# Linear attention decode with keys on partitions, masked copies, roots by token, and column-tiled products issued behind their last operand

## The chip, the cores and the metric

The kernel runs on one core of one Trainium2 chip. The metric is the device time of one execution in microseconds (us), the median of several runs. Five engines run their own instruction queues side by side: TensorE (matmuls, PE in the profile), VectorE (DVE), ScalarE (ACT), GpSimd (POOL) and SyncE (SP), which here issues every DMA transfer.

## The reference, cut to what matters

One inference step of a decoder layer, in float32, for a new prompt (16 meta tokens and 256 tokens) and for one new token each of 8 running sequences. The normalized input is projected into three branches, a state-space scan (S5), gated linear attention (GLA) and attention over a local window of 128 (SWA); their results are gated, summed and projected, and a squared-ReLU MLP follows. The change touches GLA and one product of SWA. GLA has 4 heads with keys of 128 and values of 256. Prompt and decode compute:

```
lg = log_sigmoid(a_in @ w_gate2 + b_gate2) / 16
# prompt: the same recurrence in closed form, started from zero
# decode, for each sequence n and head h:
s = exp(lg)[..., None] * s + k[..., :, None] * v[..., None, :]
o = einsum('nhd,nhdv->nhv', q, s)
# both:
o = rmsnorm(o, g_out) * silu(r)          # over the 256 values of a head
```

The new decode state `s` is an output for each of the 8 sequences, 4 x 128 x 256 floats each. SWA ends in `o = einsum(p, v)` with softmaxed scores p.

## The kernel before, in words

Features lie on the 128 partitions and tokens run along the free axis: T = 280 columns (16 meta, 256 prompt, 8 decode) or NQ = 264 without meta tokens. Every large projection goes through `linear` (L144): `Weights.half` (L109 to L118) loads half a weight tile of 512 KB (`wraw`, L112), ScalarE rounds it into a high half (`whi`, L116), VectorE subtracts for the low half (`wlo`, L117), and `accumulate` (L130) multiplies three times, high by high, high by low and low by high. Nearly all of the kernel's matmuls are these. They need nothing of the branches until the branch outputs are projected, so projections of gates and queries run while the branches are computed.

The order of each engine's queue, SP's too, is fixed when the kernel is built: a scheduler walks the program with a time model of its own and takes, at each step, the ready instruction of highest priority. Priority is program order, raised where the code says `tc.high_priority`. On the chip each queue then runs in this order and waits where an operand is late. Tiles with a tag share `bufs` buffers, and a new tile waits until the old holder of its buffer is released.

GLA comes after the value projection (L623 to L640). `vt` holds prompt values with tokens on partitions, `vdc` (L630) decode values, `lg` the log gates. Then:

- Decode rows (L665 to L676): `dec3` gathers exp(lg), k and q of the decode tokens; TensorE transposes it, and it is written to a DRAM scratch `scr1`, so that it can be read back broadcast over all partitions.
- Prompt, eight levels (L706 to L747): at each level a q product `qt` (L713, GpSimd), a k product `ek` (L720, L725, VectorE), four products per half (L732), and the result multiplied by a mask (L736) and added into the attention matrix (L737), both on VectorE. Then the prompt's outputs go into `o_t` (L785), and the prompt's final state follows through `ku` (L794), four transposes a piece (L800) and L808.
- Decode (L814 to L829): 16 rounds, 8 sequences by two pairs of heads, with values on the partitions. Each loads broadcast rows (L817) and a state `s0` of 256 KB (L819), both in two buffers; GpSimd multiplies by the decay (L820); for each head and value half VectorE adds k times v (L825) and multiplies by q with a sum into `o_t` (L827); the state is stored (L829).
- Norm (L836 to L847): squares on ScalarE (L838), their sum on GpSimd (L839), a product with a matrix of ones that leaves the sum over partitions on every partition (L841), a copy (L842), one reciprocal root over 4 x 264 columns (`rsqrt`, L170 to L176), and the scaling of `o_t` (L847).
- Later `o_t` is multiplied by the gate `sr`, fetched from DRAM (L928, GpSimd), and split into high and low halves (L929, L930) for the branch's projection.

In SWA (the loop that ends at L1088, all at a raised priority) scores are transposed (L1076), copied to `pt`, and multiplied with the values by four products on four column tiles (L1082), two heads' operands in `pts[0]` and two in `pts[1]`.

Of the kernel before, what the change touches and what calls it, by code (L numbers as in the profile page):

```python
# [16 lines left out]
KT = D // 128  # L17
# [68 lines left out]
def trunk(tc, A):  # L86
# [68 lines left out]
    def C(name):  # L155
        a, n = CONST_COLS[name]
        return cst[:, a:a + n]
# [52 lines left out]
    vt = gproj.tile([128, 3, 8, 128], F32)  # L210
    vdc = gproj.tile([128, 8, DEC], F32)
    ab = gproj.tile([32, T], F32)
# [410 lines left out]
    for mm in range(4):  # L623
        vv = []
        for j in range(2):
            ps = linear(A['w_vb'][2 * mm + j], xpair, 0, T)
            vv.append(ev_tile())
            with tc.high_priority():
                V.tensor_mul(vv[j], ps[:, :T], r1)
            V.tensor_copy(vdc[:, 2 * mm + j], vv[j][:, TP:])  # L630
        ps = ps_side('A')
# [17 lines left out]
    with tc.tile_pool(name="lgp", bufs=1, side="right") as lp:  # L649
# [10 lines left out]
        S.activation(lab, lab, AF.Ln, bias=ones[:, 0:1])  # L660
        V.tensor_sub(lg, lg, lab)
    IT = 1.0 / 16.0


    dec3 = gmain.tile([128, DEC, 2, 3, 2], F32)  # L665
    for i in range(2):
        h2 = slice(2 * i, 2 * i + 2)
        S.activation(dec3[:, :, i, 0].rearrange("p n g -> p g n"), lg[:, h2, TP:], AF.Exp, scale=IT)
        V.tensor_copy(dec3[:, :, i, 1].rearrange("p n g -> p g n"), kb[:, h2, TP:])
        V.tensor_copy(dec3[:, :, i, 2].rearrange("p n g -> p g n"), qb[:, h2, SEQ:])  # L670
    ps = ps_side()
    PE.transpose(ps[:96, :128], dec3.rearrange("p n i z g -> p (n i z g)"), ident)
    drow = gmain.tile([96, 128], F32, name="drow", tag="rows", bufs=2)
    S.copy(drow, ps[:96, :128])
    scr1 = tc.dram_tile([DEC, 2, 6 * DK], F32, name="scr1")
    SY.dma_start(scr1.rearrange("n i (z d) -> (n i z) d", d=DK), drow)  # L676

# [25 lines left out]

    lvm = C('lvmask').rearrange("p (l t) -> p l t", l=7)
    eq, ek = None, None
    for lev in range(8):  # L706
# [5 lines left out]
        S.activation(eq.rearrange("p g (b h) -> p g b h", h=h), right, AF.Exp, scale=IT)  # L712
        P.tensor_mul(qt.rearrange("p g (b h) -> p g b h", h=h), eq.rearrange("p g (b h) -> p g b h", h=h),  # L713
                     qp.rearrange("p g (b two h) -> p g b two h", two=2, h=h)[:, :, :, 1, :])
# [12 lines left out]
        if lev < 7:  # L727
            for i in range(2):
                ps = ps_side()
                psv = ps[:, :GH * 64].rearrange("p (g t) -> p g t", g=GH)  # L730
                for hd in range(GH):
                    PE.matmul(psv[:, hd], kt[:, hd, 128 * i:128 * i + 128], qt[:, hd, 64 * i:64 * i + 64],  # L732
                              start=True, stop=True)
                dst = att_tile(i).rearrange("p g (b two h) -> p g b two h", two=2, h=h)[:, :, :, 1, :]
                msk = gp.tile([128, GH, 64], F32, name="msk", tag="msk")
                V.tensor_mul(msk, psv, lvm[:, lev][:, None, :].to_broadcast([128, GH, 64]))  # L736
                V.tensor_add(dst, dst, msk.rearrange("p g (b h) -> p g b h", h=h))  # L737
        else:
# [73 lines left out]


    for n in range(DEC):  # L814
        for i in range(2):
            rows = gmain.tile([128, 3, 2, DK], F32, name="rows", tag="rows", bufs=2)
            SY.dma_start(rows, bass.AP(tensor=scr1.tensor, offset=scr1[n, i].offset, ap=[[0, 128], [1, 6 * DK]]))  # L817
            s0 = gmain.tile([128, 2, 2, DK], F32, name="s0", tag="s0", bufs=2)
            SY.dma_start(s0, A['gla0'][n, :, 2 * i:2 * i + 2])  # L819
            P.tensor_mul(s0, s0, rows[:, 0][:, :, None, :].to_broadcast([128, 2, 2, DK]))  # L820
            scrap = gmain.tile([128, DK], F32, name="scrap", tag="scrap", bufs=1)
            for j in range(2):
                for vh in range(2):
                    m = 2 * (2 * i + j) + vh
                    V.scalar_tensor_tensor(s0[:, j, vh], rows[:, 1, j], vdc[:, m, n:n + 1], s0[:, j, vh],  # L825
                                           op0=OP.mult, op1=OP.add)
                    V.scalar_tensor_tensor(scrap, s0[:, j, vh], 1.0, rows[:, 2, j], op0=OP.mult, op1=OP.mult,  # L827
                                           accum_out=o_t[:, m, SEQ + n:SEQ + n + 1])
            SY.dma_start(A['o_sgla'][n, :, 2 * i:2 * i + 2], s0)  # L829


    gpx.close()
    gp = gpx.enter_context(tc.tile_pool(name="gla5", bufs=1, side="right"))
    rg = gp.tile([128, GH, NQ], F32)
    rsv = gp.tile([128, 3, GH, NQ], F32)
    for hd in range(GH):  # L836
        sq = gp.tile([128, 2, NQ], F32, name="osq", tag="osq", bufs=2)
        S.activation(sq, o_t[:, 2 * hd:2 * hd + 2], AF.Square)  # L838
        P.tensor_add(sq[:, 0], sq[:, 0], sq[:, 1])  # L839
        ps = ps_side()  # L840
        PE.matmul(ps[:, :NQ], ones, sq[:, 0], start=True, stop=True)  # L841
        V.tensor_scalar(rsv[:, 1, hd], ps[:, :NQ], 1.0, None, op0=OP.mult)  # L842
    rsqrt(rg, rsv[:, 1], DV, rsv[:, 0], rsv[:, 2])
    for hd in range(GH):
        for vh in range(2):
            m = 2 * hd + vh
            V.scalar_tensor_tensor(o_t[:, m], o_t[:, m], g_out[:, vh:vh + 1], rg[:, hd], op0=OP.mult, op1=OP.mult)  # L847

# [76 lines left out]
    with tc.high_priority(SIDE):  # L925
        for m in range(8):
            sr = fetch(gp.tile([128, NQ], F32, name="sr", tag="sr", bufs=2), ('r', m))
            P.tensor_mul(o_t[:, m], o_t[:, m], sr)  # L928
            S.activation(yb[0][:, m], o_t[:, m], AF.Copy, scale=0.5)  # L929
# [17 lines left out]
    with ExitStack() as swx:  # L947
# [84 lines left out]
        for i in range(2):  # L1032
# [18 lines left out]
            for tt in range(2):  # L1051
# [19 lines left out]
                for z, (c0, w, vi) in enumerate(chunks):  # L1071
                    pts = []
                    for half in range(2):
# [5 lines left out]
                        pts.append(pt_)  # L1079
                    for j in range(4):  # L1080
                        rows = slice(32 * j, 32 * j + 32)
                        PE.matmul(yp[tt][rows], vtc[:w, vi, i, rows], pts[j // 2][:w],  # L1082
                                  start=z == 0, stop=z == 1, tile_position=(0, 32 * j))
            for tt in range(2):
# [199 lines left out]
def layout(i):  # L1284
# [24 lines left out]
    for r, n in enumerate(('s5_b_re', 's5_b_im')):  # L1309
# [14 lines left out]
    a['gvec'] = np.concatenate([_feat(i['gla_b_gate2'][0]), _feat(i['gla_g_out'][0])], 1)  # L1324
    a['gla0'] = i['state_gla'][0].reshape(DEC, GH, DK, 2, 128).transpose(0, 4, 1, 3, 2)
    sk = i['swa_sinks'][0]
# [10 lines left out]

OUTS = {'o_y': (128, KT, NQ), 'o_s5': (128, 2, 32, 1 + DEC), 'o_gla': (128, GH, DV), 'o_sgla': (DEC, 128, GH, 2, DK),
        'o_pk': (128, 2, WIN), 'o_pv': (128, 2, WIN), 'o_sk': (128, 2, DEC, 128), 'o_sv': (128, DEC, 256)}


def collect(r):
# [4 lines left out]
    sv = r['o_sv'].transpose(1, 0, 2).reshape(1, DEC, WIN, KVH, HD)  # L1347
    sg = r['o_sgla'].transpose(0, 2, 4, 3, 1).reshape(1, DEC, GH, DK, DV)
    out = (y[:SEQ][None], y[SEQ:][:, None], s5[0, :1][None], s5[1, :1][None],
# [22 lines left out]
```

## Time and profile before

| what | value |
|---|---|
| median of 3 runs | 1756.17 us (1754.62 to 1757.02) |
| the profiled execution | 1750.47 us |
| its span, from first to last instruction | 1748.7 us |
| mean granted TensorE clock | 0.989 |
| TensorE matmul busy | 1686.3 us (96%) |
| VectorE, ScalarE, GpSimd busy | 1134.0, 841.3, 236.0 us |

Busy times are unions of instruction spans on one engine; a busy TensorE is not TensorE at its peak, since matmuls are pipelined. An f32 matmul shows as two instructions, each with a load of its weights (PEld). The granted clock is a share of full speed: 1.0 is 2.4 GHz, 0.5 is 1.2 GHz, and a value between is a mean over a stretch with both. In a list of groups a row ends with the idle time ahead of the group on its engine, and what released it.

### The profile page before, as it was taken

The numbers are of one execution on the slowest core, as the hardware profiler recorded it, in microseconds if no ns is written. First come the engines' busy times: TensorE is split into PE (matmuls) and PEld (weight loads), VectorE is DVE, ScalarE is ACT, GpSimd is POOL, SyncE is SP. The second block draws the span as 40 slices with busy tenths as digits, with TensorE's granted clock in tenths as the row PEclk, the third lists the DMA queues.
The fourth block names the chain that finished last, engine by engine and source line by source line (L and its number), as shares of the span: only waits on it lengthen the run. The fifth ranks groups of instructions, "written<-read, shape, count | busy, mean of one in ns | idle before, by whom it ended". The sixth has DMA issues, their size and how long they took to land.

```text
span 1748.7 us, 34406 instructions
## 1 busy us (share of the span) xinstructions
PE 1686.3 (96%) x13818; PEld 1648.5 (94%) x13818; DVE 1134.0 (65%) x1941; ACT 841.3 (48%) x1267; POOL 236.0 (13%) x199
## 2 busy tenths in 40 slices
PE   7999999999989899999999899999999999999996
PEld 6998999998889888899999799999999999999996
DVE  8855999988958876745754755445544554455544
ACT  4336665645435555443445554445433453345552
POOL 2032111102222300005422500000000000000012
PEclk9999999999999999999999899999999999999998
DMA  7758787765677675467765355555555555555552
GB/s 244 248 187 277 220 221 220 224 222 162 214 240 244 206 247 199 149 198 230 232 236 183 119 174 183 183 181 181 186 181 184 180 183 181 182 181 181 182 181 97
DMA packets 135139, 346.40 MB, mean 198 GB/s; under 512 B 19083, under 2 KB 56100, under 8 KB 134468
## 3 DMA queue, kind: packets, MB, share of 16 engines
q1 hardware_dynamic: 134980, 344.21, 61.0%
q8 instruction: 108, 1.77, 0.4%
q14 instruction: 51, 0.42, 0.1%
HBM read 319.67 MB, written 24.47 MB: 197 GB/s over the span
## 4 chain that ended last, share of the span: by engine, by line
PE 77%; DMA 8%; DVE 8%; POOL 2%; issue 2%; ACT 1%; SPq 1%; POOLq 0%; DVEq 0%; ACTq 0%
PE psm L130 72%; DMA s<-gla 2%; DVE wlo L117 2%; DMA scrB<-bhl 1%; DMA cw<-s5c 1%; DMA o_sgla<-s 1%; PE psA L1082 1%; DVE s L825 1%; PE psm L141 1%; PE psB L523 1%; POOL s L820 1%; SPq L383 1%; DVE hl L1214 1%; DVE xl L227 0%; DVE scrap L827 0%
## 5 line engine op out<-in xcount | busy, mean ns | idle before, releaser
L117 DVE TENSOR_TENSOR wlo<-wraw,whi 128x1024 fp32r<-128x1024 f32 x528 | 656.0, 1244 | 279.3 <-ACT whi L116 276.0
L116 ACT CAST whi<-wraw 128x1024 fp32r<-128x1024 f32 x528 | 551.8, 1046 | 592.6 <-PE psm L130 512.3
L130 PE MATMUL psm<-xh,whi 128*128 128x264 f32 (+1 forms) x1424 | 210.0, 288 | 5.4 <-ACT whi L116 4.5
L130 PE MATMUL psm<-xh,wlo 128*128 128x264 f32 (+1 forms) x1424 | 209.9, 287 | 0.0
L130 PE MATMUL psm<-xl,whi 128*128 128x264 f32 (+1 forms) x1424 | 209.5, 288 | 0.0
L130 PEld LDWEIGHTS psm<-xh,whi 128*128 128x128 f32 x1424 | 189.1, 189 | 6.9 <-ACT whi L116 4.9
L130 PEld LDWEIGHTS psm<-xl,whi 128*128 128x128 f32 x1424 | 189.5, 190 | 1.9 <-issue 1.8
L130 PEld LDWEIGHTS psm<-xh,wlo 128*128 128x128 f32 x1424 | 188.8, 188 | 2.3 <-issue 1.9
L1188 POOL TENSOR_TENSOR sqt<-sqt 128x264 f32<-128x264 f32 x41 | 47.2, 1152 | 780.0 <-ACT sqt L1181 774.9
L130 PE MATMUL psm<-zzl,whi 128*128 128x264 f32 x1024 | 144.5, 284 | 0.0
L130 PE MATMUL psm<-zzh,wlo 128*128 128x264 f32 x1024 | 144.5, 284 | 0.0
L130 PE MATMUL psm<-zzh,whi 128*128 128x264 f32 x1024 | 144.4, 284 | 0.0
L130 PE MATMUL psm<-hh,whi 128*128 128x264 f32 x960 | 135.4, 284 | 0.0
L130 PE MATMUL psm<-hh,wlo 128*128 128x264 f32 x960 | 135.4, 284 | 0.0
L130 PE MATMUL psm<-hl,whi 128*128 128x264 f32 x960 | 135.4, 284 | 0.0
L130 PEld LDWEIGHTS psm<-zzl,whi 128*128 128x128 f32 x1024 | 132.3, 188 | 0.0
L130 PEld LDWEIGHTS psm<-zzh,wlo 128*128 128x128 f32 x1024 | 132.3, 188 | 0.0
L130 PEld LDWEIGHTS psm<-zzh,whi 128*128 128x128 f32 x1024 | 132.2, 188 | 0.0
L130 PEld LDWEIGHTS psm<-hh,wlo 128*128 128x128 f32 x960 | 123.9, 188 | 0.0
L130 PEld LDWEIGHTS psm<-hh,whi 128*128 128x128 f32 x960 | 123.9, 188 | 0.0
L130 PEld LDWEIGHTS psm<-hl,whi 128*128 128x128 f32 x960 | 123.9, 188 | 0.0
L1242 DVE SCALAR_TENSOR_TENSOR fft<-psm,r 128x264 f32<-128x264 f32 x63 | 27.1, 431 | 93.1 <-PE psm L130 93.1
(457 smaller groups left out, 2063.4 us busy)
## 6 DMA issues: line engine op xcount, KB each, us to landing
wraw<-w_ff SPq DMA_DIRECT2D x256, 512.0 KB, 3.7
wraw<-w_g SPq DMA_DIRECT2D x96, 512.0 KB, 4.7
wraw<-w_up SPq DMA_DIRECT2D x48, 512.0 KB, 4.6
wraw<-w_out SPq DMA_DIRECT2D x32, 512.0 KB, 3.7
wraw<-w_u SPq DMA_DIRECT2D x16, 512.0 KB, 6.3
wraw<-w_vb SPq DMA_DIRECT2D x16, 512.0 KB, 5.4
bst<-scrB SPq DMA_DIRECT2D x64, 128.0 KB, 4.3
wraw<-w_rb SPq DMA_DIRECT2D x16, 512.0 KB, 5.2
```

The lines of the kernel that those rows point to most:

```text
L116: S.copy(hi, raw)
L117: V.tensor_sub(lo, raw, hi.bitcast(F32))
L130: PE.matmul(ps[:, :c1 - c0], w[:, k], rhs[r][:, 8 * i + k, c0:c1], start=n == 0, stop=n == 24 * len(halves) - 1)
L141: PE.matmul(ps[m][:, :c1 - c0], w[:, k], rhs[r][:, 8 * i + k, c0:c1], start=i + k + n == 0, stop=i == 1 and k == 7 and n == 2)
L383: SY.dma_start(ff[HG * g:HG * g + HG, k // 2, k % 2], bass.AP(tensor=scrF.tensor, offset=scrF.offset + k * 4096 + g * PS, ap=[[0, HG], [8 ...
L523: PE.matmul(eps_[:, ri * NP:ri * NP + NP], bst[:, q, w, ri], ust[:, q], start=w == 0, stop=w == 1)
L820: P.tensor_mul(s0, s0, rows[:, 0][:, :, None, :].to_broadcast([128, 2, 2, DK]))
L825: V.scalar_tensor_tensor(s0[:, j, vh], rows[:, 1, j], vdc[:, m, n:n + 1], s0[:, j, vh], op0=OP.mult, op1=OP.add)
L1082: PE.matmul(yp[tt][rows], vtc[:w, vi, i, rows], pts[j // 2][:w], start=z == 0, stop=z == 1, tile_position=(0, 32 * j))
L1188: eng.tensor_add(t, total, t)
L1214: V.scalar_tensor_tensor(hl[:, m], x1[:, m], g_ffn[:, m:m + 1], hh[:, m].bitcast(F32), op0=OP.mult, op1=OP.subtract)
L1242: V.scalar_tensor_tensor(t, ps[:, :NQ], 0.0, r3, op0=OP.max, op1=OP.mult)
```

## The change

Decode of GLA puts keys on the partitions. `vdc` is laid out by sequence, transposed and written to `scr1` as value rows, in the block that computes `lg`. Each of 8 rounds, one a sequence, loads a whole state of 512 KB and the value rows broadcast (512 KB). ScalarE scales the values by k, VectorE makes the new state by one instruction a head (decay as the scalar), and TensorE reads it out: the stationary operand is a column block of `qpad`, zero but for the query of this sequence, so that four heads on four column tiles accumulate all 8 sequences in one PSUM buffer, `pso`. The last head's product is issued first and the other three behind it (`tc.issue_after`). The result is copied, transposed twice and put into `o_t`.

In the levels, the mask multiply and add become one predicated copy, and the q product goes from GpSimd to VectorE. The norm forms sums of squares by token with tokens on partitions (products with one column), takes roots of twelve columns, and broadcasts them by a product of ones with a diagonal matrix. The adds of squares and the gating of `o_t` go from GpSimd to VectorE. In SWA the four column-tiled products are issued from the last one on, which needs the later operand. The layouts of the state in and out follow.

```diff
@@ -208,7 +208,7 @@
     qb = gproj.tile([128, GH, NQ], F32)
     kb = gproj.tile([128, GH, T], F32)
     vt = gproj.tile([128, 3, 8, 128], F32)
-    vdc = gproj.tile([128, 8, DEC], F32)
+    vdc = gproj.tile([128, DEC, 8], F32)
     ab = gproj.tile([32, T], F32)
     gv = gproj.tile([128, 6], F32)
 
@@ -627,7 +627,7 @@
             vv.append(ev_tile())
             with tc.high_priority():
                 V.tensor_mul(vv[j], ps[:, :T], r1)
-            V.tensor_copy(vdc[:, 2 * mm + j], vv[j][:, TP:])
+            V.tensor_copy(vdc[:, :, 2 * mm + j], vv[j][:, TP:])
         ps = ps_side('A')
         for j in range(2):
             for i in range(2):
@@ -659,21 +659,21 @@
         S.activation(lab, lab, AF.Exp, scale=-1.0)
         S.activation(lab, lab, AF.Ln, bias=ones[:, 0:1])
         V.tensor_sub(lg, lg, lab)
+
+        ps = ps_side()
+        PE.transpose(ps[:64, :128], vdc.rearrange("p n m -> p (n m)"), ident)
+        drow = lp.tile([64, 128], F32)
+        S.copy(drow, ps[:64, :128])
+        scr1 = tc.dram_tile([DEC, 8 * 128], F32, name="scr1")
+        SY.dma_start(scr1.rearrange("n (m d) -> (n m) d", d=128), drow)
     IT = 1.0 / 16.0
 
 
-    dec3 = gmain.tile([128, DEC, 2, 3, 2], F32)
-    for i in range(2):
-        h2 = slice(2 * i, 2 * i + 2)
-        S.activation(dec3[:, :, i, 0].rearrange("p n g -> p g n"), lg[:, h2, TP:], AF.Exp, scale=IT)
-        V.tensor_copy(dec3[:, :, i, 1].rearrange("p n g -> p g n"), kb[:, h2, TP:])
-        V.tensor_copy(dec3[:, :, i, 2].rearrange("p n g -> p g n"), qb[:, h2, SEQ:])
-    ps = ps_side()
-    PE.transpose(ps[:96, :128], dec3.rearrange("p n i z g -> p (n i z g)"), ident)
-    drow = gmain.tile([96, 128], F32, name="drow", tag="rows", bufs=2)
-    S.copy(drow, ps[:96, :128])
-    scr1 = tc.dram_tile([DEC, 2, 6 * DK], F32, name="scr1")
-    SY.dma_start(scr1.rearrange("n i (z d) -> (n i z) d", d=DK), drow)
+    dk = gmain.tile([128, GH, DEC], F32)
+    S.activation(dk, lg[:, :, TP:], AF.Exp, scale=IT)
+    qpad = gmain.tile([128, GH, DEC * DEC], F32)
+    V.memset(qpad, 0.0)
+    V.tensor_copy(qpad[:, :, ::DEC + 1], qb[:, :, SEQ:])
 
     Gc = lg[:, :, META:TP]
     Hc = gmain.tile([128, GH, SEQ], F32)
@@ -701,7 +701,7 @@
     def halves_of(a, h):
         return a.rearrange("p g (b two h) -> p g b two h", two=2, h=h)
 
-    lvm = C('lvmask').rearrange("p (l t) -> p l t", l=7)
+    lvm = C('lvmask').bitcast(I32).rearrange("p (l t) -> p l t", l=7)
     eq, ek = None, None
     for lev in range(8):
         h = 1 << lev
@@ -710,7 +710,7 @@
         qt = gp.tile([128, GH, 128], F32, name="qt", tag="eq", bufs=3)
         right = halves_of(Gc, h)[:, :, :, 1, :]
         S.activation(eq.rearrange("p g (b h) -> p g b h", h=h), right, AF.Exp, scale=IT)
-        P.tensor_mul(qt.rearrange("p g (b h) -> p g b h", h=h), eq.rearrange("p g (b h) -> p g b h", h=h),
+        V.tensor_mul(qt.rearrange("p g (b h) -> p g b h", h=h), eq.rearrange("p g (b h) -> p g b h", h=h),
                      qp.rearrange("p g (b two h) -> p g b two h", two=2, h=h)[:, :, :, 1, :])
         if lev == 0:
             kt = kp
@@ -732,9 +732,8 @@
                     PE.matmul(psv[:, hd], kt[:, hd, 128 * i:128 * i + 128], qt[:, hd, 64 * i:64 * i + 64],
                               start=True, stop=True)
                 dst = att_tile(i).rearrange("p g (b two h) -> p g b two h", two=2, h=h)[:, :, :, 1, :]
-                msk = gp.tile([128, GH, 64], F32, name="msk", tag="msk")
-                V.tensor_mul(msk, psv, lvm[:, lev][:, None, :].to_broadcast([128, GH, 64]))
-                V.tensor_add(dst, dst, msk.rearrange("p g (b h) -> p g b h", h=h))
+                V.copy_predicated(dst, lvm[:, lev].rearrange("p (b h) -> p b h", h=h)[:, None]
+                                  .to_broadcast([128, GH, 64 // h, h]), psv.rearrange("p g (b h) -> p g b h", h=h))
         else:
             ps = ps_side()
             for hd in range(GH):
@@ -811,40 +810,60 @@
         SY.dma_start(A['o_gla'][:, 2 * i:2 * i + 2], sf)
 
 
+    pso = ps_side('B')
     for n in range(DEC):
-        for i in range(2):
-            rows = gmain.tile([128, 3, 2, DK], F32, name="rows", tag="rows", bufs=2)
-            SY.dma_start(rows, bass.AP(tensor=scr1.tensor, offset=scr1[n, i].offset, ap=[[0, 128], [1, 6 * DK]]))
-            s0 = gmain.tile([128, 2, 2, DK], F32, name="s0", tag="s0", bufs=2)
-            SY.dma_start(s0, A['gla0'][n, :, 2 * i:2 * i + 2])
-            P.tensor_mul(s0, s0, rows[:, 0][:, :, None, :].to_broadcast([128, 2, 2, DK]))
-            scrap = gmain.tile([128, DK], F32, name="scrap", tag="scrap", bufs=1)
-            for j in range(2):
-                for vh in range(2):
-                    m = 2 * (2 * i + j) + vh
-                    V.scalar_tensor_tensor(s0[:, j, vh], rows[:, 1, j], vdc[:, m, n:n + 1], s0[:, j, vh],
-                                           op0=OP.mult, op1=OP.add)
-                    V.scalar_tensor_tensor(scrap, s0[:, j, vh], 1.0, rows[:, 2, j], op0=OP.mult, op1=OP.mult,
-                                           accum_out=o_t[:, m, SEQ + n:SEQ + n + 1])
-            SY.dma_start(A['o_sgla'][n, :, 2 * i:2 * i + 2], s0)
+        s0 = gmain.tile([128, GH, DV], F32, name="s0", tag="s0", bufs=2)
+        SY.dma_start(s0, A['gla0'][n])
+        vb = gmain.tile([128, GH, DV], F32, name="vb", tag="vb", bufs=2)
+        SY.dma_start(vb.rearrange("p g d -> p (g d)"),
+                     bass.AP(tensor=scr1.tensor, offset=scr1[n].offset, ap=[[0, 128], [1, GH * DV]]))
+        for hd in range(GH):
+            S.activation(vb[:, hd], vb[:, hd], AF.Copy, scale=kb[:, hd, TP + n:TP + n + 1])
+            V.scalar_tensor_tensor(s0[:, hd], s0[:, hd], dk[:, hd, n:n + 1], vb[:, hd], op0=OP.mult, op1=OP.add)
+
+        def read(hd):
+            return PE.matmul(pso[32 * hd:32 * hd + DEC, :DV], qpad[:, hd, n * DEC:n * DEC + DEC], s0[:, hd],
+                             start=n == 0, stop=n == DEC - 1, tile_position=(0, 32 * hd))
+
+        with tc.issue_after(read(GH - 1).ins):
+            for hd in range(GH - 1):
+                read(hd)
+        SY.dma_start(A['o_sgla'][n], s0)
+    od = gmain.tile([128, DV], F32, name="od", tag="vb", bufs=2)
+    V.memset(od, 0.0)
+    for hd in range(GH):
+        S.copy(od[32 * hd:32 * hd + DEC], pso[32 * hd:32 * hd + DEC, :DV])
+    ps = ps_side()
+    for vh in range(2):
+        PE.transpose(ps[:, 128 * vh:128 * vh + 128], od[:, 128 * vh:128 * vh + 128], ident)
+    V.tensor_copy(o_t[:, :, SEQ:].rearrange("p (g v) n -> p g v n", v=2),
+                  ps[:, :256].rearrange("p (v g n) -> p g v n", v=2, g=GH)[:, :, :, :DEC])
 
 
     gpx.close()
     gp = gpx.enter_context(tc.tile_pool(name="gla5", bufs=1, side="right"))
-    rg = gp.tile([128, GH, NQ], F32)
-    rsv = gp.tile([128, 3, GH, NQ], F32)
+
+    psn = ps_side()
     for hd in range(GH):
         sq = gp.tile([128, 2, NQ], F32, name="osq", tag="osq", bufs=2)
         S.activation(sq, o_t[:, 2 * hd:2 * hd + 2], AF.Square)
-        P.tensor_add(sq[:, 0], sq[:, 0], sq[:, 1])
+        V.tensor_add(sq[:, 0], sq[:, 0], sq[:, 1])
+        for c, c0 in enumerate((0, 128, NQ - 128)):
+            PE.matmul(psn[:, 3 * hd + c:3 * hd + c + 1], sq[:, 0, c0:c0 + 128], ones[:, 0:1],
+                      start=hd + c == 0, stop=hd == GH - 1 and c == 2)
+    rsg = gp.tile([128, 3, 3 * GH], F32)
+    rsqrt(rsg[:, 0], psn[:, :3 * GH], DV, rsg[:, 1], rsg[:, 2])
+    for hd in range(GH):
+        dg = gp.tile([128, NQ], F32, name="dgo", tag="dgo", bufs=2)
+        r_ = [rsg[:, 0, 3 * hd + c:3 * hd + c + 1] for c in range(3)]
+        V.tensor_scalar(dg[:, :128], ident, r_[0], None, op0=OP.mult)
+        S.activation(dg[:, 128:256], ident, AF.Copy, scale=r_[1])
+        V.tensor_scalar(dg[:, 256:], ident[:, 256 - NQ:], r_[2], None, op0=OP.mult)
         ps = ps_side()
-        PE.matmul(ps[:, :NQ], ones, sq[:, 0], start=True, stop=True)
-        V.tensor_scalar(rsv[:, 1, hd], ps[:, :NQ], 1.0, None, op0=OP.mult)
-    rsqrt(rg, rsv[:, 1], DV, rsv[:, 0], rsv[:, 2])
-    for hd in range(GH):
+        PE.matmul(ps[:, :NQ], ones, dg, start=True, stop=True)
         for vh in range(2):
             m = 2 * hd + vh
-            V.scalar_tensor_tensor(o_t[:, m], o_t[:, m], g_out[:, vh:vh + 1], rg[:, hd], op0=OP.mult, op1=OP.mult)
+            V.scalar_tensor_tensor(o_t[:, m], o_t[:, m], g_out[:, vh:vh + 1], ps[:, :NQ], op0=OP.mult, op1=OP.mult)
 
     for m in range(KT):
         ps = linear(A['w_g'][m], xpair, META, T)
@@ -925,7 +944,7 @@
     with tc.high_priority(SIDE):
         for m in range(8):
             sr = fetch(gp.tile([128, NQ], F32, name="sr", tag="sr", bufs=2), ('r', m))
-            P.tensor_mul(o_t[:, m], o_t[:, m], sr)
+            V.tensor_mul(o_t[:, m], o_t[:, m], sr)
             S.activation(yb[0][:, m], o_t[:, m], AF.Copy, scale=0.5)
             V.scalar_tensor_tensor(yb[1][:, m], o_t[:, m], 0.5, yb[0][:, m].bitcast(F32),
                                    op0=OP.mult, op1=OP.subtract)
@@ -1077,10 +1096,14 @@
                         pt_ = sp.tile([128, 512], F32, name="pt", tag="pt", bufs=3)
                         S.copy(pt_[:w], ps[:w])
                         pts.append(pt_)
-                    for j in range(4):
+                    def pv(j):
                         rows = slice(32 * j, 32 * j + 32)
-                        PE.matmul(yp[tt][rows], vtc[:w, vi, i, rows], pts[j // 2][:w],
-                                  start=z == 0, stop=z == 1, tile_position=(0, 32 * j))
+                        return PE.matmul(yp[tt][rows], vtc[:w, vi, i, rows], pts[j // 2][:w],
+                                         start=z == 0, stop=z == 1, tile_position=(0, 32 * j))
+
+                    with tc.issue_after(pv(3).ins):
+                        for j in (1, 2, 0):
+                            pv(j)
             for tt in range(2):
                 yv = yp[tt].rearrange("p (j t) -> p j t", j=4)
                 c = slice(128 * tt, 128 * tt + 128)
@@ -1322,7 +1345,7 @@
-    a['gla0'] = i['state_gla'][0].reshape(DEC, GH, DK, 2, 128).transpose(0, 4, 1, 3, 2)
+    a['gla0'] = i['state_gla'][0].transpose(0, 2, 1, 3)
...
```

## Rows read from the trace of the kernel before

**Rows 1.** The page's first part: busy time and share of the span by engine.

```profile
PE 1686.3 (96%) x13818; PEld 1648.5 (94%) x13818; DVE 1134.0 (65%) x1941; ACT 841.3 (48%) x1267; POOL 236.0 (13%) x199
```

**Rows 2.** Busy time by stretch: engines with counts, granted clock, DMA share, GB/s.

```profile
395.00:470.00 75.00, 68.47 (x547) 67.68 (x546) 67.78 (x136) 36.18 (x45) 19.46 (x15) 0.95 0.56 181
470.00:540.00 70.00, 64.15 (x456) 60.68 (x455) 47.38 (x149) 25.20 (x35) 13.79 (x11) 0.95 0.78 260
540.00:612.00 72.00, 62.48 (x486) 60.34 (x485) 61.62 (x104) 40.37 (x65) 25.70 (x21) 0.98 0.63 202
...
620.00:750.00 130.00, 130.00 (x1018) 112.63 (x1018) 91.64 (x219) 68.79 (x153) 0.77 (x2) 1.00 0.56 188
...
420.00:430.00 10.00, 10.00 (x64) 10.00 (x64) 10.00 (x25) 3.82 (x5) 1.77 (x1) 0.73 0.47 146
```

**Rows 3.** TensorE's waits, 385 to 760 us: total us, times, longest.

```profile
PE psB L800 <- DVE ku L794: 5.9, 1, 5.9
PE psB L994 <- DMA qf<-scrP: 4.1, 1, 4.1
PE psA L732 <- DVE ek L720: 3.6, 1, 3.6
PE psm L130 <- ACT whi L116: 2.2, 1, 2.2
PE psB L841 <- POOL osq L839: 2.1, 2, 1.3
PE psA L741 <- DVE ek L725: 1.6, 1, 1.6
PE psm L130 <- ACT ev L904: 0.9, 1, 0.9
PE psB L732 <- DVE ek L720: 0.9, 1, 0.9
```

**Rows 4.** The chain that ended last, 484 to 502 us: start, us, what.

```profile
486.33 4.04 DMA o_sgla<-s
...
490.43 4.48 DMA s<-gla
```

**Rows 5.** Waits of VectorE and GpSimd, 385 to 620 us.

```profile
POOL s L820 <- DMA s<-gla: 55.4, 8, 12.8
...
DVE s L825 <- POOL s L820: 26.7, 11, 5.9
```

**Rows 6.** TensorE's instructions in order of time: start, us, instruction, count.

```profile
670.92 1.05 PE L1082 MATMUL psA<-pt,vtc 128*32 128x512 f32 x4
671.90 0.66 PE L1076 MATMUL psB<-cst,sc 128*128 128x128 f32 x4
...
724.14 1.07 PE L1082 MATMUL psA<-pt,vtc 128*32 128x512 f32 x8
725.14 1.12 PE L130 MATMUL psm<-xl,whi 128*128 128x264 f32 x7
```

**Rows 7.** The same view later: decode of local attention, and a later norm.

```profile
746.46 1.07 PE L1119 MATMUL psA<-vd,pdt 128*32 128x256 f32 x16
...
1001.94 2.06 PE L1167 MATMUL psA<-ones,sqt 128*128 128x1 f32 x18
```

**Rows 8.** VectorE's groups by shape, 385 to 610 us: busy us, mean ns.

```profile
L825 DVE SCALAR_TENSOR_TENSOR s<-rows,vdc,s 128x128 f32<-128x128 f32 x64 | 23.8, 430 | 26.7 <-POOL s L820 26.7
L827 DVE SCALAR_TENSOR_TENSOR scrap<-s,rows 128x128 f32<-128x128 f32 x64 | 23.2, 362 | 0.7
...
L173 DVE RECIPROCAL rg<-rsv 128x1056 f32<-128x1056 f32 x1 | 6.8, 6753 | 0.8 <-ACT rsv L171 0.8
L886 DVE TENSOR_TENSOR ev<-psm,r 128x264 f32<-128x264 f32 x15 | 6.4, 424 | 0.8 <-PE psm L130 0.8
```

**Rows 9.** GpSimd's groups by shape, 385 to 610 us.

```profile
L928 POOL TENSOR_TENSOR o_t<-o_t,sr 128x264 f32<-128x264 f32 x8 | 12.0, 1515 | 7.5 <-DMA sr<-scrP 6.7 <-DVE o_t L847 0.8
```

More of the change, by code (lines that the diff above doesn't have):

```diff
@@ L1335, in layout @@
     return {k: np.ascontiguousarray(v, dtype=np.float32) for k, v in a.items()}
-OUTS = {'o_y': (128, KT, NQ), 'o_s5': (128, 2, 32, 1 + DEC), 'o_gla': (128, GH, DV), 'o_sgla': (DEC, 128, GH, 2, DK),
+OUTS = {'o_y': (128, KT, NQ), 'o_s5': (128, 2, 32, 1 + DEC), 'o_gla': (128, GH, DV), 'o_sgla': (DEC, 128, GH, DV),
         'o_pk': (128, 2, WIN), 'o_pv': (128, 2, WIN), 'o_sk': (128, 2, DEC, 128), 'o_sv': (128, DEC, 256)}
@@ L1347, in collect @@
     sv = r['o_sv'].transpose(1, 0, 2).reshape(1, DEC, WIN, KVH, HD)
-    sg = r['o_sgla'].transpose(0, 2, 4, 3, 1).reshape(1, DEC, GH, DK, DV)
+    sg = r['o_sgla'].transpose(0, 2, 1, 3)[None]
     out = (y[:SEQ][None], y[SEQ:][:, None], s5[0, :1][None], s5[1, :1][None],
```

## The prediction

> **What bounds the kernel now.** I read the page first: TensorE's matmuls are busy 96% of the span, VectorE 65%, ScalarE 48%, GpSimd 13% [rows 1]. So an edit can pay in only two ways: less matmul time, or less time in which TensorE waits or runs at a low clock. The table by stretch shows where the second kind lies. In local attention, 620 to 750 us, TensorE is busy 130.00 of 130.00 us, while the three stretches that hold linear attention, from 395 to 612 us, have 6.53, 5.85 and 9.52 us idle, 21.9 in all, and granted clocks of 0.95, 0.95 and 0.98 [rows 2]. Idle and clock belong together: after one wait of 3.6 us (below) the slice 420 to 430 is granted 0.73, that is partly the lower of the two levels. As an estimate the lower clock costs (1 - 0.95) x 68.47 + (1 - 0.95) x 64.15 + (1 - 0.98) x 62.48 = 7.8 us of matmul time in these three stretches.
>
> The list of TensorE's waits names the causes [rows 3], and I sort them by what they stand behind.
> - **A**, 2.1 us: the normalization's matmul (L841) waits for GpSimd's add (L839).
> - **B**, 5.9 + 3.6 + 1.6 + 0.9 = 12.0 us: products and transposes of the prompt wait for VectorE (ku L794, ek L720 and L725). The chain of waits shows why ku is late: a decode state is stored in 4.04 us, the next loaded into the freed buffer in 4.48 us, then GpSimd multiplies, then VectorE runs its decode lines, and ku stands behind these in VectorE's queue [rows 4]. VectorE waited 26.7 us in 11 pieces for that GpSimd line, and it 55.4 us in 8 pieces for the load [rows 5].
> - **C**, 4.1 + 2.2 + 0.9 = 7.2 us: the end of the stage, where SP's fetches, VectorE's low halves of weights and ScalarE's high halves come late behind GpSimd's gating of o_t (L928).
>
> With the lower clock (3.4 + 3.2 = 6.6 us to B, 1.2 to C) these are A 2.1, B 18.6, C 8.4, together 29.1 us. That is all that waiting can give back.
>
> **The change part by part: matmul time.** Four terms, all in stretches where TensorE has nothing to spare.
>
> Local attention's product with the values (L1082) leaves 64 rows, since an f32 product shows as two instructions: 32 products. They stand mostly in blocks of four rows, two products on two column tiles. One block starts at 670.92 and the next instruction at 671.90: 0.98 us. Once two such halves met, and eight rows on four column tiles took from 724.14 to 725.14: 1.00 us [rows 6]. The new order issues all four when the later of their two operands is there. So 64/4 = 16 blocks x 0.98 = 15.7 us become 8 x 1.00 = 8.0 us: -7.7 us. Nothing hides this gain or takes it, since TensorE is never idle there. Its bounds are 0 (if other matmuls are put between the four) and -7.7.
>
> The decode read-out moves from VectorE to TensorE: 8 samples x 4 heads, 256 columns, four column tiles at once. The nearest row is the decode of local attention (L1119): 16 rows, two groups of four products with 256 columns, 1.07 us, so 0.54 a group [rows 7]. 8 x 0.54 = +4.3 us; if each four ran one behind the other, four times that, +17.1.
>
> The sums of squares by token are 4 heads x 3 pieces = 12 products with one column, 24 rows. The kernel's other norms hold the same shape: L1167, 18 rows in 2.06 us, 0.114 each [rows 7]. 24 x 0.114 = +2.7 us. The weights to be loaded, not the column, seem to set this. The Trainium skill's TensorEngine Tiling (Array Packing), section Instruction Overhead, gives a matmul with one column the cost of some 60 cycles; by that, 25 ns at 2.4 GHz, the term would be about 0.6 us and the sum 2.1 us lower. I keep the row.
>
> The transpose of decode rows is replaced by one of values (even). Two transposes of the result are new: four stand in 0.66 us at 671.90 [rows 6], so +0.3 us. The four products with ones that broadcast the root replace four of the same width. Sum of the matmul terms: -7.7 + 4.3 + 2.7 + 0.3 = -0.4 us. The two big edits pay for each other.
>
> **The change part by part: waiting.** VectorE's decode work was 64 + 64 instructions, 23.8 + 23.2 = 47.0 us [rows 8]. Now it is 32 updates of 256 columns; the nearest width is 264 columns at 0.424 us (L886), so 32 x 0.424 = 13.6 us; the slowest end, twice the 128-column 0.430, is 27.5. The root over 1056 columns, with its 6.8 us reciprocal (L173), shrinks to twelve columns. VectorE takes over GpSimd's q products, square sums and gating: the last was 1.515 us a step on GpSimd (L928) [rows 9] and should cost VectorE about the 0.424 of the same 264 columns. Masks by predicated copy replace a multiply and an add by one instruction; the trace has none, so I bound it between nothing and the two it replaces, and count a gain of nothing. In all VectorE loses some 30 us of work (47.0 - 13.6, the root and the work taken over about even) in a stretch where it is busy 67.78 of 75 us [rows 2]. That by itself is worth nothing to the end; it counts only where something of A, B or C stood behind it.
>
> ScalarE gains 32 scalings of the broadcast values, about 13 us at the same 0.42. It is busy half the span [rows 1] and that covers them. If the cover fails, the high halves of weights are late, as in the 2.2 us row of [rows 3]. One PSUM buffer of three in its group is held through the decode; four of the five side buffers stay for the levels, so I count nothing (the dearest case is one more wait like the 3.6 us of ek).
>
> DMA: 16 loads of states, 16 of rows and 16 stores become 8, 8 and 8, with larger pieces. SP, which issues these in one queue with the weights, has 24 fewer to wait for. The store, load, compute loop through two buffers is run 4 times a buffer instead of 8. The values row is written out earlier too: it needs only the value projections, not the gates. What is new, and against the change: each sample's four products now stand in TensorE's own queue, and everything behind them waits if the update is late. In the old kernel no matmul but L841 at the end depended on a decode load. ScalarE, too, now waits for the broadcast.
>
> How much of the 29.1 us goes? The lower bound is nothing, the upper all of it. I take half, 14.5 us: A and C lose the GpSimd step they stood behind; B has half the rounds, but the rounds that stay now stand before TensorE as well. Sum: -14.5 - 0.4 = -14.9 us. The profiled execution took 1750.47 us (span 1748.7), so 1735.6 by its scale. The median of the runs is 5.7 us above it, and I apply the difference there: 1756.17 - 14.9 = 1741.3 us. From no change the runs here can tell about 0.2%, 3.5 us.
>
> **The rivals.**
> 1. All waiting goes: VectorE has so much room that nothing is late. 1756.17 - 29.1 - 0.4 = 1726.7 us. For it: each named releaser loses its work. Against: waits of C come from SP's queue and its fetches, which stay.
> 2. Nothing of it goes: the order of each queue is fixed when the kernel is built, and a new order puts as many waits elsewhere. 1755.8 us. For it: waits as short as 0.9 us are spread over many instructions. Against: B's two long ones have one visible cause.
> 3. Slower: TensorE waits at each read-out for its state, as VectorE did. VectorE's mean wait was 26.7/11 = 2.43 us [rows 5]; 8 x 2.43 = 19.4 us, and two of them long enough to lower the clock, at (1 - 0.73) x 10 = 2.7 us each: 24.8. It replaces B's 18.6 while A and C stay: +6.2 - 0.4, 1762.0 us. It decides from 2.4 us a read-out on, clock included; (18.6 + 0.4)/8. For it: a 5.9 us wait let no matmul of the projections through. The Trainium skill, TensorE: Matmul & The Clock Gate, section Part 3: Packing small matmuls, says that matmuls start and end strictly in program order; this trace agrees. Against: there are half as many rounds, and they start earlier.
> 4. The four products are not packed: the edit only keeps three behind the fourth, and other matmuls may stand between. The 7.7 us stay unearned, 1749.0 us; if the read-outs fall apart into pairs too, another 4.3, 1753.3.
>
> **How the numbers follow.** Forecast 0.48 (its own range, from a fifth to five sixths of the 29.1: 1732 to 1750), rival 1 0.12, rival 2 0.14, rival 3 0.15, rival 4 0.11. The range 1726 to 1759 takes in rival 1 at its lower edge, rivals 2 and 4, and leaves rival 3 and the outer end of rival 1 out. Faster: the forecast, rival 1 and most of rival 4, 0.70; within 0.2%: rival 2 and the rest, 0.15; slower: 0.15.
>
> **What would show it.** In the changed profile: L1082's line in blocks of eight rows, some 8.6 us busy instead of 16.8; read-outs in blocks of eight rows at about 0.54 us; TensorE's idle time in the linear attention stretch near 11 us, with a granted clock of 0.97 or more; no waits of matmuls on GpSimd lines; VectorE near 30 us lighter there. It would be wrong if waits of the read-out product lead the list of TensorE's waits, if the predicated copies or the broadcasts hold up VectorE or ScalarE, or if the reordered queues open waits after 620 us, where there were none.

## The result, and the profile after

The changed kernel takes 1726.34 us (median of 4 runs, 1725.61 to 1727.7), the kernel before 1755.39 us beside it: ratio 0.9836, 95% interval 0.9819 to 0.9853, some 29 us. The forecast was 1741. The sign held and so, by a hair, did the lower edge of the range (1726); the size did not: the gain is nearly twice the forecast's. One execution of the old kernel in a later run, 2340.49 us at a mean granted clock of 0.658, is left out of all ratios.

By stretch of the changed kernel's trace (columns as in [rows 2]):

```profile
395.00:470.00 75.00, 74.15 (x609) 72.34 (x607) 61.55 (x95) 46.68 (x64) 1.00 (x2) 1.00 0.61 197
470.00:540.00 70.00, 69.08 (x550) 63.85 (x549) 34.84 (x52) 34.96 (x55) 1.71 (x2) 1.00 0.74 256
540.00:612.00 72.00, 70.99 (x579) 69.12 (x578) 56.05 (x113) 47.63 (x87) 6.63 (x7) 1.00 0.75 242
620.00:750.00 130.00, 129.66 (x1092) 120.30 (x1091) 89.34 (x206) 71.32 (x150) 0.77 (x2) 1.00 0.59 189
```

Where TensorE was idle for 21.9 us it now is for 0.85 + 0.92 + 1.01 = 2.8, and the granted clock is 1.00 throughout, so the estimated 7.8 us of lower clock are gone too. With the clock's part an estimate, that is 26.9 us. The list of TensorE's waits, 380 to 760 us, answers to [rows 3]; nothing longer than 1.0 us is left of it:

```profile
PE psB L1013 <- DMA qf<-scrP: 1.0, 1, 1.0
PE psB L825 <- DVE s L822: 0.9, 1, 0.9
```

The matmul terms, from TensorE's groups. First local attention's product in the old kernel (385 to 760 us):

```profile
L1082 PE MATMUL psA<-pt,vtc 128*32 128x512 f32 (+1 forms) x64 | 16.8, 603 | 0.0
```

Then the changed kernel's groups of 375 to 760 us (the same product, now L1101; the read-out; the sums by token; the transposes of the result):

```profile
L1101 PE MATMUL psA<-pt,vtc 128*32 128x512 f32 (+1 forms) x64 | 8.5, 603 | 0.0
...
L825 PE MATMUL psB<-s,qpad 128*8 128x256 f32 x64 | 4.8, 381 | 0.9 <-DVE s L822 0.9
...
L852 PE MATMUL psB<-ones,osq 128*128 128x1 f32 x24 | 2.8, 243 | 0.0
...
L838 PE MATMUL psB<-cst,od 128*128 128x128 f32 x2 | 0.4, 270 | 0.0
```

16.8 - 8.5 = 8.3 us less against 4.8 + 2.8 + 0.4 = 8.0 more: -0.3, where -0.4 was worked out. In order of time the read-outs stand in blocks of eight rows (the first two rounds' sixteen together), one of which waited:

```profile
515.49 0.62 PE L825 MATMUL psB<-s,qpad 128*8 128x256 f32 x8 [0.92 <-DVE s L822]
```

VectorE's groups that answer to [rows 8], and its one new kind, the predicated copy; its wait for the decode's operands was 26.7 us [rows 5]. In the three stretches VectorE is busy 24 us less than before:

```profile
L822 DVE SCALAR_TENSOR_TENSOR s<-s,dk,vb 128x256 f32<-128x256 f32 x32 | 13.4, 478 | 3.4 <-DMA s<-gla 3.1 <-ACT dk L673 0.3
...
L735 DVE COPY_PREDICATED att<-cst,psB 128x256 f32<-128x256 int32 x9 | 4.7, 548 | 1.4 <-PE psB L732 1.4
```

The span shrank from 1748.7 to 1724.6 us, 24.1. Idle time, clock and matmuls add up to 27.2; the lower clock is only an estimate, and the start of the MLP lost about a microsecond. The median fell by 5 us more than the span, since the median of the old kernel's runs lies 4.9 us above its profiled execution.

### The profile page after: what moved, and what is told of

Its sections match the earlier page's. It is cut to its first block, busy times and chain, and to the rows that moved or that the text cites. A ratio compares the mean times of both kernels' runs of the same rounds, so it can differ in the third digit from the quotient of the medians.

```text
span 1724.6 us, 34358 instructions
## 1 busy us (share of the span) xinstructions
PE 1681.4 (97%) x13908; PEld 1649.3 (96%) x13908; DVE 1097.0 (64%) x1791; ACT 857.6 (50%) x1306; POOL 188.8 (11%) x163
## 4 chain that ended last, share of the span: by engine, by line
PE 82%; DVE 7%; DMA 6%; issue 1%; ACT 1%; SPq 1%; POOL 1%; POOLq 0%; ACTq 0%; DVEq 0%
PE psm L130 76%; DVE wlo L117 2%; DMA scrB<-bhl 1%; SPq L383 1%; PE psm L141 1%; DMA vb<-scr 1%; DMA cw<-s5c 1%; PE psB L523 1%; DMA wraw<-w_qc 1%; DMA sr<-scrP 1%; DVE hl L1237 1%; DMA wraw<-w_up 1%; DVE xl L227 1%; ACT whi L116 0%; PE psA L1101 0%
```

## The experiments

All ratios are to the kernel before on the same chip. V, G, W and so on name theories as they stood before each run. For three runs (rounds, VectorE's load, three GpSimd steps back) the changed kernel has no time on the same chip; their distance to it is given twice, by times and by ratios.

**One part alone: local attention's order.** The old kernel with

```diff
-                    for j in range(4):
-                        PE.matmul(yp[tt][rows], ..., tile_position=(0, 32 * j))
...
+                    with tc.issue_after(pv(3).ins):
+                        for j in (1, 2, 0):
+                            pv(j)
```

> The old kernel with one edit, the order of local attention's four column-tiled products. Theory 1 (matmul time is gained one for one where TensorE is never idle): L1082's busy time falls from 16.8 to about 8.6 us and the time by 7.7 us, ratio 0.9956. Rival (other matmuls stand between the four, or the gain is given back as waiting later): the line stays above 13 us busy, or the time moves by less than 3 us.

1745.31 us, ratio 0.9948 (0.9926 to 0.997): -9.1 us, with the 7.7 well inside. The product's line is busy 8.5 us instead of 16.8, and the other waits stayed (ku 5.9, ek 3.6 us). Theory 1 holds.

**One part alone: the new decode.** The old kernel with the new decode (`s0`, `vb`, `qpad`, `pso`) and roots by token, without the rest; the old norm beside the new decode does not fit in memory, so what the roots by token do by themselves is not known.

> The old kernel with the new decode and the roots by token, but masks, q products, square sums and gating as before (three of them on GpSimd), and local attention as before. Matmul terms +4.8 + 2.8 + 0.4 = 8.0 us. Theory V (the waits of linear attention stood behind the old decode in VectorE's queue): B's 18.6 us go, A and C stay, sum -10.6 us, ratio 0.994. Theory G (the GpSimd steps are as much a cause): B goes by half at most, sum 0 to -2 us, ratio 0.999 to 1.000.

Ratio 0.9949 (0.9929 to 0.9968), -9.0 us. The second and third stretch, and TensorE's longest wait, at the end of the stage as C's were:

```profile
470.00:540.00 70.00, 69.48 (x548) 63.53 (x547) 35.31 (x52) 34.02 (x53) 2.15 (x2) 1.00 0.72 260
540.00:612.00 72.00, 65.76 (x510) 63.15 (x510) 51.55 (x96) 45.42 (x86) 19.10 (x19) 0.95 0.66 220
...
PE psB L1014 <- ACT KH L984: 5.6, 1, 5.6
```

As theory V had it: B gone, C still there. But the new decode has no GpSimd step either, so this run does not tell its layout from the going of that step. With the 8.0 us of new matmuls, 17 us of waiting went.

**The complement.** Masked copies, roots by token and the three GpSimd steps (L713, L839, L928) on VectorE, with the old decode.

> The old kernel with masked copies, roots by token and the three GpSimd steps moved to VectorE, but the old decode and the old local attention. Matmul term +2.8 us. Theory V: A and C go (10.5 us), B's 18.6 stay, since the old decode still stands in VectorE's queue: sum -7.7 us, ratio 0.9956. Theory G: B goes by half and more as well: sum -17 us or beyond, ratio 0.990.

Ratio 0.9934 (0.9914 to 0.9954), -11.6 us, between the two. 540 to 612 us is full (72.00 of 72.00); 395 to 470 has 1.55 us idle instead of 6.53, which theory V did not expect, as the old decode was still in VectorE's queue; 470 to 540 has 8.66.

**The old kernel again.**

> The old kernel unchanged, for a second profile: its first profiled execution took 1750.5 us where ordinary runs took 1753 to 1757. Theory V and theory G both expect the time unchanged, ratio 1.000. If the second profile is at 1754 to 1757 and the extra 5 us lie in waits between 395 and 612 us, the first profile showed too little of what there was to gain; if they lie elsewhere, the median cannot be compared with that profile's waits one for one.

Ratio 0.9988 (0.9974 to 1.0002). The second profile took 1751.42 us with the same waits (ku 6.1, ek 3.4, L994 3.2 us). Its other runs but one lie between 1749.7 and 1757.7; what the slower ones add, no trace shows.

**Rounds.** The changed kernel with two heads and 256 KB a round:

```diff
     for n in range(DEC):
+        for i in range(2):
+            h2 = slice(2 * i, 2 * i + 2)
...
-        SY.dma_start(s0, A['gla0'][n])
+            SY.dma_start(s0, A['gla0'][n, :, h2])
```

> The changed kernel with its decode in 16 rounds of two heads and 256 KB, as many rounds and DMA issues as the old decode had, the same arithmetic. Theory W (few rounds keep the read-outs from waiting): TensorE waits at read-outs by 5 us and more, 8 more groups of two products cost 4 us of matmul time at the most, time 1735 or more. Theory V (it is VectorE's and GpSimd's lighter queues): waits at read-outs stay under 2 us, time 1727 to 1731.

1732.18 us, ratio 0.9887 (0.9866 to 0.9907), against 0.9836: +6 us by times, +9 by ratios. But no read-out waited; TensorE is idle for 0.53 us from 395 to 612, at a clock of 1.00. VectorE waited 12.1 us for the states, in 7 pieces, and TensorE for none of it. So theory W fell on its waits. The read-outs, now in pairs, are busy 9.7 us instead of 4.8; with 2.3 us less idle time that about accounts for the profiled execution, which took 1728.36 us. The other three took 1732 to 1735; what they add stays open.

**VectorE's load.** The changed kernel with, in each round,

```diff
+        for k in range(2):
+            for hd in range(GH):
+                for vh in range(2):
+                    V.scalar_tensor_tensor(scrap, s0[:, hd, ...], 1.0, vb[:, hd, ...], ..., accum_out=acc1)
```

> The changed kernel with VectorE's old decode load put back: in each round 16 products of 128 columns with a sum, on the new state and the scaled values, results thrown away (128 in all, as the old decode had, some 46 us). Theory V: B comes back at least by half, time 1736 to 1746, with waits of TensorE for VectorE lines of the prompt or for the read-out's state. Theory W: no more than 3 us, time under 1730.

1731.52 us, ratio 0.9878 (0.9852 to 0.9903), +5 us by times and +7 by ratios against the changed kernel's 0.9836, with intervals that touch. VectorE is busy 68.82 of 75 us in the first stretch, more than in the old kernel, and TensorE 75.00 of 75:

```profile
395.00:470.00 75.00, 75.00 (x619) 73.56 (x618) 68.82 (x161) 44.58 (x61) 1.05 (x2) 1.00 0.59 194
```

Read-outs waited 3.7 us in all. This profiled execution was the fastest, 1724.73 us, while the other three took 1730 to 1733, so no trace shows what the load costs in those. By the times it is less than half of B: a full VectorE is a small part of the cause.

**Three GpSimd steps back.** The changed kernel with

```diff
-        V.tensor_mul(qt.rearrange("p g (b h) -> p g b h", h=h), ...
+        P.tensor_mul(qt.rearrange("p g (b h) -> p g b h", h=h), ...
-        V.tensor_add(sq[:, 0], sq[:, 0], sq[:, 1])
+        P.tensor_add(sq[:, 0], sq[:, 0], sq[:, 1])
-            V.tensor_mul(o_t[:, m], o_t[:, m], sr)
+            P.tensor_mul(o_t[:, m], o_t[:, m], sr)
```

> The changed kernel with q products, square sums and the gating of o_t back on GpSimd. Theory V: A and C come back, 10.5 us, time 1737, with waits at the end of the stage (the bias product of local attention, the first projection behind it) and B still gone. Theory G: more than that, since the q products return too: 1742 or more, with waits at the levels' products.

1733.96 us, ratio 0.9901 (0.9881 to 0.9922), +8 us by times and +11 by ratios. C is back, and a little at the levels:

```profile
PE psB L1013 <- DMA relb<-rel_bias: 4.7, 1, 4.7
PE psB L732 <- POOL qt L713: 1.4, 1, 1.4
```

**One GpSimd step back, in the decode.** With the changed kernel and two more variants on one chip:

> The changed kernel itself, on the same chip as the next three, as their yardstick: ratio 0.984 to the kernel before if it is the same here.

1725.77 us, ratio 0.9839 (0.9818 to 0.9861).

```diff
...
+            P.tensor_mul(s0[:, h2], s0[:, h2], dk[:, h2, n:n + 1].to_broadcast([128, 2, DV]))
-            V.scalar_tensor_tensor(s0[:, hd], s0[:, hd], dk[:, hd, n:n + 1], vb[:, hd], ...)
+            V.tensor_add(s0[:, hd], s0[:, hd], vb[:, hd])
```

> The changed kernel with a GpSimd step put back between the load and VectorE: the decay multiply of the state on GpSimd (two of 512 columns a round, 16 in all, as the old decode had), and VectorE only adds. Theory Q (VectorE's queue stood behind the GpSimd step of each round, 26.7 us, and the prompt's lines behind that): VectorE's wait for GpSimd comes back, 10 us and more, and TensorE waits at prompt products or read-outs, time up by 8 us or more against the changed kernel. Theory V (load, or something else in the layout): VectorE's work is even, so under 3 us.

1737.84 us, ratio 0.9912 (0.9888 to 0.9936): +12.1 us beside the changed kernel. TensorE's longest wait and the second stretch:

```profile
PE psB L828 <- POOL s L822: 3.5, 1, 3.5
...
470.00:540.00 70.00, 65.88 (x493) 60.00 (x491) 31.89 (x40) 31.37 (x51) 12.03 (x11) 0.95 0.67 234
```

The price is theory Q's, its mechanism only in part: a read-out waited 3.5 us behind the GpSimd step, but VectorE waited only 3.2 us for GpSimd. VectorE's update, now an add, took 668 ns a piece where the changed kernel's took 478.

**Late rows.** The changed kernel with

```diff
...
+        V.scalar_tensor_tensor(vdl, lg[:, 0, :64], 0.0, vdc.rearrange("p n m -> p (n m)"), ...)
-        PE.transpose(ps[:64, :128], vdc.rearrange("p n m -> p (n m)"), ident)
+        PE.transpose(ps[:64, :128], vdl, ident)
```

> The changed kernel with the value rows transposed and written out only once the log gates are there (one VectorE instruction more that reads them), as late as the old rows were. Theory R (the early rows took away the first wait): the first round waits for the broadcast again, up by 3 to 6 us with a wait at the levels' products. Theory Q: under 2 us, since the loads that follow set the pace.

1726.12 us, ratio 0.984 (0.9826 to 0.9855): 0.4 us beside the changed kernel. The early rows earn nothing that these runs can tell.

**The same step taken out of the old kernel.** One letter:

```diff
-            P.tensor_mul(s0, s0, rows[:, 0][:, :, None, :].to_broadcast([128, 2, 2, DK]))
+            V.tensor_mul(s0, s0, rows[:, 0][:, :, None, :].to_broadcast([128, 2, 2, DK]))
```

> The old kernel with one word changed: the decay multiply of its decode (L820) on VectorE instead of GpSimd, 16 x about 0.68 us more for VectorE. Theory Q: the queue of VectorE waits for the load itself, 1.3 us sooner each round; B falls by half or more, time down by 6 to 12 us, ratio 0.993 to 0.997. Theory V: more load on VectorE, so the same or slower, ratio 1.000 or above.

1744.1 us, ratio 0.9942 (0.9926 to 0.9957): -10 us, a third of the whole gain. Again the time came as expected and VectorE's wait did not fall as expected: 20.7 us for loads and issue instead of 26.7. Yet TensorE waited 2.6 us for ku instead of 5.9 and 1.1 for ek instead of 3.6, and VectorE's own lines became faster: L825 took 354 ns a piece instead of 430, L827 322 instead of 362.

**All four GpSimd steps out of the old kernel.** The letter of the last experiment and, as in the diff of the three steps read backwards, L713, L839 and L928 from `P` to `V`, nothing else; then the same with local attention's order.

> The old kernel with four words changed: its GpSimd steps in linear attention (q products, decode decay, square sums, gating) on VectorE, nothing else. VectorE then carries some 24 us more than before in this stage. Theory P (the GpSimd steps are what the waits stood behind): it earns the most of 29.1 us by itself, time 1731 to 1738, ratio 0.986 to 0.990. Rival (the lighter VectorE queue of the new decode is needed as well): VectorE becomes the limit, with waits of projections for low halves and of prompt products, time 1742 or more.

1736.34 us, ratio 0.9903 (0.9887 to 0.9919), -17 us. By stretch:

```profile
395.00:470.00 75.00, 75.00 (x625) 74.42 (x624) 68.31 (x147) 42.02 (x52) 0.99 (x2) 1.00 0.65 212
470.00:540.00 70.00, 67.68 (x506) 64.16 (x504) 51.66 (x158) 27.68 (x39) 1.62 (x2) 1.00 0.79 265
540.00:612.00 72.00, 68.49 (x539) 67.42 (x540) 68.81 (x124) 40.69 (x60) 6.98 (x7) 0.98 0.65 215
```

VectorE is busier than in [rows 2], and TensorE's idle time is 5.83 us instead of 21.9.

> The same four words and local attention's new order. No decode read-out and no sums by token on TensorE, so 8.0 us of matmul time less than in the changed kernel. Theory P: 1722 to 1730, level with the changed kernel or ahead of it. Rival: 1733 or more.

1723.96 us, ratio 0.9836 (0.982 to 0.9852): the whole gain, without the new decode, the masked copies and the roots by token.

**What the rest adds.** The changed kernel with the old decode, its decay on VectorE; the changed kernel with the S5 gate's `P.tensor_add(z, ...)` on VectorE.

> The changed kernel with the old decode, whose decay multiply runs on VectorE; masked copies, roots by token and the other moved steps stay. Matmul terms 5.2 us less than the changed kernel. Theory P: 1722 to 1728. Rival: waits at ku and at the levels come back through VectorE's decode lines, 1732 or more.

1728.39 us, ratio 0.9873 (0.9853 to 0.9892): behind the old kernel with the four moved steps and local attention's order (old_four_pv) by 0.37%, between the two expectations, with ku's wait back at 4.3 us.

> The changed kernel with the last GpSimd step of the neighbourhood moved too, the eight adds in the S5 gate (z, 1.0 us each). Theory P, taken further: waits left at the end of the stage fall, 1723 to 1726. Rival: no wait stands behind these adds, within 2 us of the changed kernel's 1726.

1724.02 us, ratio 0.9833 (0.9817 to 0.985): not to be told from the changed kernel.

**Side by side.**

> The old kernel with five words changed (the four GpSimd steps and the adds in the S5 gate on VectorE) and local attention's new order. Theory P: 2 us below old_four_pv, 1722, and ahead of the changed kernel by 3 to 5 us. Rival (VectorE is too full): level with old_four_pv or behind, 1724 to 1730.

> The same with masked copies in the levels, which spare VectorE some 5 us. Theory P: 1719 to 1722, the fastest. Rival (these instructions do not stand in front of a wait any more): within 1 us of five_pv.

> The changed kernel as the yardstick on the same chip: ratio 0.984.

1723.27 us (0.9828, 0.981 to 0.9845), 1727.53 (0.9856, 0.9837 to 0.9875) and 1725.56 (0.9838, 0.9819 to 0.9857). Five letters and local attention's order are level with the whole change: 2.3 us ahead, inside the intervals. The masked copies on top were expected to gain and cost 4 us (no run of one kernel reaches into the other's; the intervals touch), with ku's wait at 4.2 us against 2.0 in the profiled executions, the slowest run of the one and nearly the slowest of the other. No version here clearly beats the changed kernel.

## Why the prediction was wrong, by its own steps

**Matmul terms: right.** -7.7, +4.3, +2.7 and +0.3 were -8.3, +4.8, +2.8 and +0.4. On the one-column products the trace decided against the rule that was weighed: 2.8/24 = 0.117 us a row, not 25 ns. The two big edits do pay for each other. Of the other signs, VectorE is 24 us lighter where near 30 were expected, and a block of read-outs takes 0.62 us where 0.54 were.

**The stretch and the size of what waiting could give: right.** 21.9 us idle and an estimated 7.8 of lower clock were there to be had, and the changed kernel has 2.8 and none.

**"I take half, 14.5 us": the step that failed.** The term measured about 27 in the trace. Rival 1's time, 1726.7, was met, but for the most part not by its mechanism (VectorE has so much room): VectorE's load put back cost 5 to 7 us (dve_load). The working put the long waits of B down to the rounds of store, load and VectorE's decode lines. It saw GpSimd's step among them, but took the going of GpSimd steps as a gain for A and C alone, and kept half because the rounds that remain stand before TensorE. Three runs contradict it. Twice the rounds made no read-out wait (rounds16). VectorE as full as in the old kernel leaves TensorE 75.00 of 75 busy from 395 to 470 us (dve_load, old_four_dve). And VectorE can wait some 20 us for decode loads while the time falls by 10 (old_decode_dve). What decided the most of it was four GpSimd steps, in B as well as in A and C. Out of the old kernel they give 17 us; one of them in the new decode costs 12, the other three 8 to 11. With local attention's 9 us that makes 26 of the 29; both in one kernel give the whole 29 (old_four_pv).

The new decode takes away waiting too. With the roots by token it took 17 us (decode_roots), where moving the one step of the old decode gained 10 (old_decode_dve); the 7 us between them about equal the 8.0 us of matmuls that it brings. So it ends level with four letters, and which of its parts earns those 7 us is not shown.

**Which part of a GpSimd step does it** is only partly shown. Two things are seen: the step is long (1.39 us against VectorE's 0.69), and it slows VectorE. The decay multiply on GpSimd in the old kernel, then on VectorE in old_four_dve (0.84 us a piece in old_decode_dve, beside the three GpSimd steps left):

```profile
L820 POOL TENSOR_TENSOR s<-s,rows 128x512 f32<-128x512 f32 x16 | 22.2, 1389 | 87.4 <-DMA s<-gla 55.4 <-ACT whi L116 8.7 <-DMA sr<-scrP 8.5
...
L820 DVE TENSOR_TENSOR s<-s,rows 128x512 f32<-128x512 f32 x16 | 11.1, 691 | 19.6 <-DMA s<-gla 18.6 <-DMA rows<-scr 0.8 <-issue 0.2
```

A line of the old decode, first in the old kernel, then in old_four_pv (minimum, median and maximum in ns; L827 goes from 273/282/1385 to 276/291/305):

```profile
L825 DVE SCALAR_TENSOR_TENSOR s<-rows,vdc,s x64: 335/344/1373, 414.6 to 546.9; 128x128 f32<-128x128 f32 x64
...
L825 DVE SCALAR_TENSOR_TENSOR s<-rows,vdc,s x64: 343/350/357, 417.4 to 555.4; 128x128 f32<-128x128 f32 x64
```

In the old kernel twelve of these 128 instructions took from 0.8 to 1.4 us, some 10.6 us in all above their medians, and each of the twelve began while a GpSimd instruction ran; in old_four_pv none of them took longer than 0.36 us. The Trainium skill, GPSIMD Engine Reference, section Key points, says that GpSimd shares its SBUF interfaces with VectorE and contends with VectorE instructions that have two SBUF inputs; the rows agree. The stretched lines stand in front of TensorE's two longest waits of B. Four of L825, which took 1.14 us undisturbed, took 3.16 us right before ek, while GpSimd ran L713 from 414.55 and L820 from 415.80; TensorE stood still for 3.6 us from 416.1 on. Before ku they took 2.14 us at 496.42.

```profile
414.63 3.16 DVE L825 SCALAR_TENSOR_TENSOR s<-rows,vdc,s 128x128 f32<-128x128 f32 x4 [1.39 <-POOL s L820]
...
484.80 1.14 DVE L825 SCALAR_TENSOR_TENSOR s<-rows,vdc,s 128x128 f32<-128x128 f32 x4 [2.86 <-POOL s L820]
```

So the stretch can be 2.0 us of the one wait and 1.0 us of the other, and the step's own length comes on top. How much each of the two brought was not tried by itself, nor whether the order fixed beforehand had counted them. That the order matters as such is an argument: masked copies leave VectorE 7 us less busy from 395 to 612 us, and the kernel with them took 4 us longer (five_pv_masks).

**Rival 2** fell: of 21.9 us idle 2.8 are left. **Rival 3** fell: one read-out waited, 0.9 us. **Rival 4** fell: all of local attention's products were packed.

## What to carry to other kernels

Where a queue's long wait is named after the engine ahead of it, try the engine assignment first: one letter in the old kernel, worth 10 us, told more than the account of rounds, loads and queues. Two edits that trade matmul time can cancel and hide that the gain comes from a third, so run the smallest edits alone before crediting the large one. Products on different column tiles gain by being issued together, behind the operand that comes last, where TensorE is full.

## What the runs showed of the hardware that was not expected

In the old kernel a GpSimd step over 512 columns beside VectorE stretched single VectorE instructions from 0.34 to 1.37 us. Four f32 products with 512 columns on four column tiles took about as long as two, 1.07 against 1.05 us. A predicated copy of 256 columns out of PSUM took 0.50 to 0.55 us, more than the 0.41 of the multiply that it replaced, and less than that and its add of 0.49 together.
